# The gating projection's second block product taken apart into seven small ones

## The chip, the cores and the metric

The kernel runs on one NeuronCore of one Trainium2 chip. The metric is the device time of one execution in microseconds (us). Three timed runs of the kernel before gave 791.55, 791.96 and 792.16 us; the median is 791.96 us.

## The reference

A transformer layer over 512 tokens of width 2048: windowed attention with its output projection, then a gated embedding, then a last norm. The attention's inner part is left out here, since neither the code of it nor its place changes.

```python
D_MODEL, SEQ, PLE_DIM = 2048, 512, 256

def rmsnorm(x, g):
    y = x * lax.rsqrt(jnp.mean(x * x, axis=-1, keepdims=True) + EPS)
    return y * g

def reference(...):
    hn = rmsnorm(x, norm_g[0])
    y = swa_mixer(hn, ...)             # ends in (out * silu(gate)) @ w_out, 512x2048 @ 2048x2048
    x = x + y
    emb = p[0] @ ple_proj[0]           # 512x256 @ 256x2048
    g = jax.nn.sigmoid(rmsnorm(x, ple_norm[0]) @ ple_gate[0])   # 512x2048 @ 2048x2048
    x = x + emb * g
    return rmsnorm(x, final_g)
```

## The kernel before, in words

**Precision.** All is fp32. A product of two fp32 tiles is three matmuls (`mm3`, lines 124 to 126): each operand is split into a rounded high part and the rest, and high x high, low x high and high x low are added in PSUM. One matmul has a 128x128 stationary tile of activations and 512 columns of weights.

**Pieces.** A weight matrix is used in pieces of 128x1024 elements (512 KB). A piece is loaded by DMA, ACT casts it into its high part (`bhi`, line 689) and DVE subtracts that for the low part (`blo`, line 690). `Pieces` (object `B`) keeps a list of them in the order of use; `get` issues the loads and splits a few pieces ahead. The raw pieces live in `wraw` (3 buffers, names `braw`) or in `grown` (8 buffers, names `ring` or `grown`), the parts in `whi` and `wlo` (3 buffers each); while the list is between two marks (`FOURTH`) every fourth piece has its parts in a tile called `spare`. The waits on these buffers, and no clock, set when a load or a split really starts.

**Block products.** Both large projections (`w_out`, then `ple_gate`) are cut into two by two blocks and made of seven block products instead of eight. The products have numbers 1 to 7; product 1 is a11 times b11, product 2 is a12 times b21, and the others use sums of blocks. A block product is eight steps `(p, jj, m)` of one piece and twelve matmuls each. The sums of weights that it needs are made ahead in HBM while attention runs, each by one copying DMA on the SP queue and one adding DMA on the POOL queue, a few slots later (`sum_weights`, lines 654 and 652); for `ple_gate` part of them is added in the tile itself ("grow": product 7's piece becomes product 6's, and that product 4's, by an adding DMA of POOL, line 671).

**Small products.** In the `w_out` stage, product 2 and product 4 are themselves seven small block products of a 128-row by 512 by 512 shape. A small product is two steps of one piece and six matmuls each ("m" and "n" in the list `OUT`), and they stand between the larger steps.

**The `ple_gate` stage** is seven whole block products in the order `ORDER_PLE` = 2, 7, 1, 6, 5, 3, 4. Products 1, 6, 5 and 3 add up in the same four PSUM banks (`chain`); product 2's result (copied to `s2` by ACT) and product 7's (`s7`) are joined on DVE by `gate`. The names of a trace are: `g` for the banks, `fhg` and `flg` for the two parts of the activations (made by `Forms` from the transposed quarters `hT`), `e` for the embedding's product, `last` and `low` for the last product's weights, split earlier by `split_last`. `gated` makes the sigmoid (ACT), the product with the embedding and the addition to x (DVE, lines 1271 and 1272) and the square for the last norm (ACT).

**Order.** PE's and SP's instructions stand as the code is written. DVE's, ACT's and POOL's stand so too inside `manual_schedule`; elsewhere the framework's scheduler orders them when the program is built. In the kernel before they are as written from the second product of the `ple_gate` stage on (`written()`).

Lines named below: 113, 107 (split of the earlier weights), 484, 492, 503 (attention's masks on POOL), 525 (the matmul that uses them), 1288 (stores).

Of the kernel before, what the change touches and what calls it, by code (L numbers as in the profile page):

```python
# [55 lines left out]
def trunk_kernel(ctx: ExitStack, tc: tile.TileContext, a: dict):  # L56
# [531 lines left out]
    ORDER_OUT, ORDER_PLE = (1, 7, 2, 6, 5, 3, 4), (2, 7, 1, 6, 5, 3, 4)  # L588
# [11 lines left out]
    def small_piece(kh, jj, i):  # L600
        return block("w_out", 2, 1, jj, 2 * kh + i)
# [23 lines left out]

    small_sum(2, 7, lambda i: small_piece(0, 1, i), lambda i: small_piece(1, 1, i))
# [19 lines left out]
    SUM_REST = 2 * len(copies) + 6 - SUM_START  # L646

    def sum_weights(i):

        if i % 2 == 0 and i // 2 < len(copies):  # L650
            if copies[i // 2]:
                nc.sync.dma_start(*copies[i // 2])
        elif i % 2 == 1 and 0 <= i // 2 - 3 < len(adds):
            nc.gpsimd.dma_start(*adds[i // 2 - 3], accum_op=ALU.add, max_dma_last_dim=8192)

    class Pieces:
# [46 lines left out]
        def ahead(self, i):  # L703

            last = len(self.specs) - 9
            for n in range(max(i, 0), min(i + REACH, last) + 1):
# [7 lines left out]
                if sooner or n <= i + 3:  # L714
                    self._prepare(n)
# [4 lines left out]
        def get(self, i):  # L720
# [3 lines left out]
            if kind in ("seed", "grow"):  # L724
                n = next((n for n in range(i + 1, len(self.specs)) if self.specs[n][2] == key), None)
                if n is not None:
                    self.due.append((i + 6, partial_of(self._prepare, n)))
# [5 lines left out]
    FIRST_RING, LAST_RING, REACH = 4, 68, 9  # L733
    FOURTH = 6, 68
    FINAL_G = 6
# [34 lines left out]
    def small_forms(ahead):  # L770

        v = lambda r, c: gates[2 + c][:, :, r * P : (r + 1) * P]
        v11, v12, v21, v22 = v(0, 0), v(0, 1), v(1, 0), v(1, 1)
        t, t5 = (fg[:, n * 512 : (n + 1) * 512].rearrange("p (k t) -> p k t", k=4) for n in range(2))
        for n, q in enumerate(ORDER_IN):
# [6 lines left out]
            fh, fl = (w[:, n % 2].rearrange("p (k t) -> p k t", k=4) for w in (pTh, pTl))  # L782
# [22 lines left out]
    OUT += SHARED  # L805

    def add_stage(nm, order):
# [23 lines left out]
        def add_embeds(p, jj):  # L831
            if nm == "ple_gate" and p in (1, 5, 3, 4):
                j = jj + 2 * (p in (5, 3))
                B.add("proj", a["ple_proj"].rearrange("(k p) d -> p k d", p=P)[:, :, j * 512 : (j + 1) * 512])

        for p in order:
            for jj in range(2):
                if nm == "ple_gate" and (p, jj) == (4, 0):
                    for v in range(2):
                        at["e", v] = len(B.specs)  # L840
                        add_embeds(p, v)
                at[p, jj] = len(B.specs)
                for m in range(4):
                    if (nm, p) in SUMS:
                        src = summed[nm, p, jj, m]
                    else:
                        src = block(nm, *{1: (1, 1), 2: (2, 1), 3: (2, 2), 6: (1, 1), 4: (2, 1)}[p], jj, m)
                    growing = 7, 6, 4
                    kind = "seed" if p == growing[0] else "grow" if p in growing else "one"
                    B.add(kind, src, (nm, jj, m) if p in growing else None)  # L850
                if p != 4:
                    add_embeds(p, jj)
        return at

    add_stage(inside.nm, ORDER_OUT)
    at_ple = add_stage("ple_gate", ORDER_PLE)

    class Forms:
# [6 lines left out]
        def steps(self, p):  # L865

            self.made[p] = []
            for h in range(2):
# [7 lines left out]
                else:  # L876
                    src, sub = {
                        2: (a12, None), 7: (a21, (a21, a11)), 1: (a11, None), 6: (a21, (a22, a21)),
# [156 lines left out]
    def banks(p, jj, nm):  # L1035
# [3 lines left out]
        tag = ("to" if p == 7 or (nm, p) == ("o", 2) else "sp")[jj]  # L1039
# [7 lines left out]
    def some_later(parts):  # L1047

        for _ in range(-(-len(later) // parts)):
            later.pop(0)()  # L1050

    def unit(p, jj, at, forms, todo):

        ps = banks(p, jj, forms.nm)
        f = forms.made[p]
        first = p not in (6, 5, 3)
        for m in range(4):
            bh, bl = B.get(at[p, jj] + m)
# [5 lines left out]
            some_later(4 - m)  # L1064
            todo()
        return ps

# [40 lines left out]
    ple_first = ple_forms.steps(2)  # L1108
# [38 lines left out]
    def inner_part(p, forms, tags):  # L1147

        x = None
        for q in ORDER_IN:  # L1150
            if q in (1, 7, 2, 4):
                ps = bank(f"o{p}_{q}", tags[q])
# [3 lines left out]
            for i in range(2):  # L1156
# [5 lines left out]
                if i == 1:  # L1162
                    coming.append(partial_of(add_in, p, q, ps))
                yield

    def add_in(p, q, ps):
        whither = {
            1: [((0, 0), -1)], 2: [((0, 0), 1)], 7: [((1, 1), 1), ((1, 0), -1)], 6: [((1, 0), -1)],
            5: [((1, 1), 1)], 3: [((0, 1), 1)], 4: [((1, 0), 1)],
        }[q]  # L1170
        for (r, c), sign in whither:
# [16 lines left out]
    smalls = small_forms(small_made)  # L1188
# [12 lines left out]
    }  # L1201
    extra[7, 0, 2] = extra[7, 1, 0] = [smalls]
# [8 lines left out]
    made, inner, seen = {}, inner_part(4, inside.made, {1: "t", 4: "t", 7: "o", 2: "o"}), 0  # L1211
    inner2, seen2 = inner_part(2, small_made, {1: "t", 7: "t", 2: "o", 4: "o"}), 0
    ahead = {p: out_forms.steps(n) for p, n in zip((1, 7, 6, 5), (7, 6, 5, 3))}
    for at, step in enumerate(OUT):
# [30 lines left out]
        if step == FINAL_G:  # L1245
            nc.sync.dma_start(fg, a["final_g"].partition_broadcast(P))
# [11 lines left out]
    def embed(t, w, tag, c=slice(0, 512)):  # L1258
        e_ps = bank(f"e{t}_{done[t]}", tag)
        for k in range(2):  # L1260
            mm3(e_ps[:, c], pTh[:, k, blk(t)], pTl[:, k, blk(t)], w[0][k][:, c], w[1][k][:, c], k == 0, k == 1)
        return e_ps

    def gated(t, j, zin, z, e_ps, c=slice(0, 512)):
# [7 lines left out]
        nc.vector.tensor_add(xt, xt, z)  # L1272
# [29 lines left out]
    s2, s7 = partial("s2"), partial("s7")  # L1302
    turns = [(kp, 1) for kp in range(4)]

    def gate(p, jj, ps, e):

        zs = []
        for tb in range(2):
            v2, v7 = s2[:, jj, tb], s7[:, jj, tb]
            if p == 2:  # L1310
                nc.scalar.copy(v2, ps[tb])
            elif p == 7:
                nc.scalar.copy(v7, ps[tb])
            elif p == 1:
                nc.vector.tensor_sub(v2, v2, ps[tb])
                zs.append((tb, jj, v2, v2))
# [9 lines left out]
    def gate_later(*v):  # L1326
        zs = gate(*v)
        if zs:
            z, y = zs
            later[:0] = [lambda: (next(z), next(y)), lambda: next(z), lambda: next(y), lambda: (run(z), run(y))]  # L1330

    rooms4 = {}
    early = {(6, 1, 2): 0, (5, 0, 2): 1, (5, 0, 3): 2, (5, 1, 2): 3, (5, 1, 3): 4, (3, 0, 3): 5, (3, 1, 2): 6}
# [10 lines left out]
    for n, p in enumerate(ORDER_PLE[:-1]):  # L1346
        nxt = ple_forms.steps(ORDER_PLE[n + 1])
        if n == 1:
            written()
        for jj in range(2):  # L1350
            calls = iter(range(4))

            def todo():
                k = early.get((p, jj, next(calls)))
                if turns:
                    turn(*turns.pop(0), "t")
                    if not turns:
                        nc.vector.tensor_reduce(ss2, ssq2, axis=AX.X, op=ALU.add)
                        run(rsqrt_mean(rstd2, ss2, D, "r2"))
                    return  # L1360
                next(nxt, None)
                if p == 2:
                    next(nxt, None)
                if k is not None:
                    split_last(k)

# [177 lines left out]
```

## Time and profile before

| what | value |
|---|---|
| median of 3 runs | 791.96 us (791.55 to 792.16) |
| the profiled execution | 791.93 us |
| its span, first to last instruction | 790.2 us |
| PE (TensorE) busy | 780.0 us, 99% |
| PEld (weight load) busy | 652.3 us, 83% |
| DVE (VectorE) busy | 612.9 us, 78% |
| ACT (ScalarE) busy | 499.6 us, 63% |
| POOL (GpSimd) busy | 175.8 us, 22% |
| mean granted TensorE clock | 0.996 |

Engines: PE is the matrix engine, PEld its weight loads, SP the engine that issues most DMAs. Times are us from the start of the span unless marked ns. Line numbers (L690) are those of the kernel before. "out<-in" names the tiles written and read, xN counts instructions. A busy matmul row is 390 ns long because matmuls are pipelined; how often one starts is read from the starts. An `idle before` time names what ended the wait. The `ple_gate` stage begins at 604.3 us and PE's last matmul starts at 781.0 us.

### The profile page before, as it was taken

The page shows a single profiled execution, that of the slowest core. Times are in us where ns is not written, and L with a number is a line of the kernel's source. Part 1 is how long each engine was busy: PE and PEld are TensorE (multiplying, and loading weights), DVE is VectorE, ACT ScalarE, POOL GpSimd, SP SyncE. Part 2 cuts the span into 40 slices and gives each one's busy share as a digit, 9 for nine tenths or more (in the row PEclk, how much of TensorE's full clock was granted, in tenths as well). Part 3 has the DMA queues.
Part 4 walks back from the last instruction along what each step waited for, and adds up shares of the span by engine and source line. Part 5 has one row for each costly group of instructions (what it writes and reads, how often), then busy time and mean ns, then how long its engine had stood idle before and what let it go on. Part 6 is the DMA issues. An engine that isn't in the chain of part 4 may idle for free.

```text
span 790.2 us, 11240 instructions
## 1 busy us (share of the span) xinstructions
PE 780.0 (99%) x3738; PEld 652.3 (83%) x3738; DVE 612.9 (78%) x1043; ACT 499.6 (63%) x1016; POOL 175.8 (22%) x382
## 2 busy tenths in 40 slices
PE   9999999999999999999999999999999999999995
PEld 8888888888888888888888888888888888888885
DVE  4445478887877788687887799999788757999886
ACT  5641376666666666565666656767679756667755
POOL 0012413554344414442243200100000120200000
PEclk9999999999999999999999999999999999999998
DMA  8781999999999998999998687997783995885433
GB/s 334 279 227 39 322 267 295 269 290 269 328 253 290 255 281 212 268 259 276 290 271 220 159 313 257 271 381 264 239 297 105 370 225 207 164 217 197 169 107 107
DMA packets 48490, 194.41 MB, mean 246 GB/s; under 512 B 7296, under 2 KB 7936, under 8 KB 42704
## 3 DMA queue, kind: packets, MB, share of 16 engines
q1 hardware_dynamic: 39456, 148.94, 53.2%
q0 software_dynamic: 8688, 44.36, 29.4%
q8 instruction: 29, 0.48, 0.3%
q10 hardware_dynamic: 288, 0.39, 0.2%
q14 instruction: 29, 0.24, 0.1%
HBM read 187.85 MB, written 70.31 MB: 327 GB/s over the span
## 4 chain that ended last, share of the span: by engine, by line
PE 98%; DMA 0%; DVE 0%; ACT 0%; issue 0%; DVEq 0%
PE gps L124 7%; PE gps L125 7%; PE gps L126 7%; PE qps L124 7%; PE qps L125 7%; PE qps L126 7%; PE o L126 6%; PE o L124 6%; PE o L125 6%; PE g L126 6%; PE g L125 6%; PE g L124 6%; PE s L401 2%; PE o L523 2%; PE vps L228 2%; PE pt L479 2%
## 5 line engine op out<-in xcount | busy, mean ns | idle before, releaser
L124 PE MATMUL gps<-xh,whi 128*128 128x512 f32 x256 | 100.7, 393 | 0.0
L125 PE MATMUL gps<-xl,whi 128*128 128x512 f32 x256 | 100.1, 391 | 0.0
L126 PE MATMUL gps<-xh,wlo 128*128 128x512 f32 x256 | 100.0, 391 | 0.0
L503 POOL TENSOR_SCALAR_AFFINE_SELECT own<-r 64x256 fp32r<-64x256 f32 x96 | 62.4, 650 | 162.3 <-ACT r L484 80.2
L113 DVE TENSOR_TENSOR wlo<-wraw,whi 128x1024 fp32r<-128x1024 f32 x60 | 73.5, 1226 | 24.7 <-ACT whi L107 23.2
L124 PE MATMUL qps<-xh,whi 128*128 128x512 f32 x224 | 87.8, 392 | 0.0
L125 PE MATMUL qps<-xl,whi 128*128 128x512 f32 x224 | 87.5, 391 | 0.0
L126 PE MATMUL qps<-xh,wlo 128*128 128x512 f32 x224 | 87.5, 390 | 0.0
L461 ACT ACTIVATE t<-t,sm 128x129 f32<-128x129 f32 x128 | 50.6, 397 | 51.2 <-DVE sm L452 47.9
L124 PE MATMUL g<-bhi,fhg 128*128 128x512 f32 x192 | 75.3, 392 | 0.0
L126 PE MATMUL g<-bhi,flg 128*128 128x512 f32 x192 | 74.9, 390 | 0.0
L125 PE MATMUL g<-blo,fhg 128*128 128x512 f32 x192 | 74.8, 389 | 0.0
L107 ACT CAST whi<-wraw 128x1024 fp32r<-128x1024 f32 x60 | 62.2, 1037 | 15.7 <-DMA wraw<-in_w_q 9.5
L689 ACT CAST bhi<-braw 128x1024 fp32r<-128x1024 f32 x44 | 46.4, 1057 | 36.1 <-PE g L126 20.5
L690 DVE TENSOR_TENSOR blo<-braw,bhi 128x1024 fp32r<-128x1024 f32 x44 | 54.1, 1229 | 18.5 <-ACT bhi L689 18.3
L690 DVE TENSOR_TENSOR blo<-ring,bhi 128x1024 fp32r<-128x1024 f32 x48 | 58.3, 1223 | 6.6 <-ACT bhi L689 6.2
L689 ACT CAST bhi<-ring 128x1024 fp32r<-128x1024 f32 x48 | 50.2, 1050 | 20.4 <-PE o L126 16.8
L126 PEld LDWEIGHTS gps<-xh,wlo 128*128 128x128 f32 x256 | 48.1, 188 | 10.5
L484 ACT CAST r<-pt 128x256 fp32r<-128x256 f32 x64 | 23.8, 372 | 51.3 <-PE pt L479 50.9
L124 PEld LDWEIGHTS gps<-xh,whi 128*128 128x128 f32 x256 | 48.1, 188 | 9.0
L125 PEld LDWEIGHTS gps<-xl,whi 128*128 128x128 f32 x256 | 48.1, 188 | 8.7
L671 POOL DMA_DIRECT2D grown<-in_ple_gate x16 | 13.7, 854 | 176.4 <-DMA grown<-ple_gate 119.8
(265 smaller groups left out, 1988.7 us busy)
## 6 DMA issues: line engine op xcount, KB each, us to landing
w_out<-in_w_out POOLq DMA_DIRECT2D x32, 512.0 KB, 8.7
wraw<-in_w_gate_in SPq DMA_DIRECT2D x32, 512.0 KB, 7.3
ring<-w_out SPq DMA_DIRECT2D x32, 512.0 KB, 5.9
wraw<-in_w_q SPq DMA_DIRECT2D x28, 512.0 KB, 8.1
braw<-in_ple_gate SPq DMA_DIRECT2D x24, 512.0 KB, 4.0
ring<-in_w_out SPq DMA_DIRECT2D x18, 512.0 KB, 4.5
w_out<-in_w_out SPq DMA_DIRECT2D x16, 512.0 KB, 9.6
w_out<-w_out SPq DMA_DIRECT2D x16, 512.0 KB, 13.6
```

The source lines that it names most:

```text
L107: nc.scalar.copy(hi, self.raw[i])
L113: nc.vector.tensor_sub(lo, raw, hi.bitcast(F32))
L124: nc.tensor.matmul(ps, sh, mh, start=first, stop=False, skip_group_check=more)
L125: nc.tensor.matmul(ps, sh, ml, start=False, stop=False, skip_group_check=more)
L126: nc.tensor.matmul(ps, sl, mh, start=False, stop=last, skip_group_check=more)
L228: nc.tensor.matmul(v_ps[t], h[:, c], both[:, :, 256:512], start=f, stop=e, skip_group_check=True)
L401: nc.tensor.matmul(s_ps[:, u, : 2 * n], st, key[:, :, first : first + n], start=True, stop=True)
L461: nc.scalar.activation(su, su, AF.Exp, bias=sm[:, u : u + 1], accum_out=sm[:, 2 + u : 3 + u])
L484: nc.scalar.copy(r[:, 0], PT[i])
L503: nc.gpsimd.affine_select(out=cols(own[places[g % 2 ^ low]]), in_=cols(r[here, low].bitcast(F32)), pattern=[[sign * QB, 2], [0, GROUP], [s ...
L689: nc.scalar.copy(hi, raw)
L690: nc.vector.tensor_sub(lo, raw, hi.bitcast(F32))
```

## The change

Product 2 of the `ple_gate` stage is taken out of the order of the large products and is made of seven small ones, as product 2 of `w_out` is already. Its fourteen "m" steps stand between the steps of products 7 (second half), 6 and 5. With that:

- eight more sums of weights are made in HBM (`small_g`, two each for small products 7, 5, 6 and 4); four sums (`ple_gate` product 5, second half) leave the time of attention and are issued in the `w_out` stage (`LATE_AT`), and the first half of product 5's sums goes to the head of the list.
- the small products' results are added by DVE in a tile `c11`, which is the tile of `final_g` (`fg`); product 1's negative is put there first by ACT. `final_g` is loaded later for that reason, in product 3.
- the embedding's steps ("e") of products 1 and 5 come later in the list.
- for x tiles (2, 2), (2, 3), (3, 2), (3, 3) the addition of the gated embedding to x is an adding DMA of POOL, no longer a DVE instruction; their squares come eight steps later.
- pieces are loaded up to seven steps ahead with at most three waiting; `spare` serves until piece 99.
- `written()` is called after product 3 only, so that the scheduler orders DVE, ACT and POOL in the whole stage up to the last product.

```diff
-    ORDER_OUT, ORDER_PLE = (1, 7, 2, 6, 5, 3, 4), (2, 7, 1, 6, 5, 3, 4)
+    ORDER_PLE = (1, 7, 6, 5, 3, 4)
...
+    large_sum("ple_gate", 5, (0,))
     small_sum(2, 7, lambda i: small_piece(0, 1, i), lambda i: small_piece(1, 1, i))
...
+    small_sum("g", 7, lambda i: gate_piece(0, 1, i), lambda i: gate_piece(1, 1, i))
+    small_sum("g", 5, lambda i: gate_piece(0, 0, i), lambda i: gate_piece(0, 1, i))
...
+    small_sum("g", 6, lambda i: small["g", 7, i], lambda i: gate_piece(0, 0, i))
...
-    large_sum("ple_gate", 5, (0,))
+    small_sum("g", 4, lambda i: small["g", 6, i], lambda i: gate_piece(1, 0, i))
...
+    LATE_SUMS = len(copies)
     large_sum("ple_gate", 5, (1,))
+    late_sums = [(c, v) for c, v in zip(copies[LATE_SUMS:], adds[LATE_SUMS:])]
+    del copies[LATE_SUMS:], adds[LATE_SUMS:]
...
+    LATE_AT = ((1, 0, 0), (1, 0, 2)), (8, 10), (9, 11), (10, 12)
...
-    FIRST_RING, LAST_RING, REACH = 4, 68, 9
-    FOURTH = 6, 68
+    FIRST_RING, LAST_RING, REACH, AHEAD, GROW = 4, 68, 9, 7, 12
+    FOURTH = 6, 100
...
+    PLE = [(1, n // 4, n % 4) for n in range(8)]
+    for n in range(8):
+        PLE.append((7, n // 4, n % 4))
+        if n >= 4:
+            PLE.append("m")
+    for n in range(8):
+        PLE += [(6, n // 4, n % 4), "m"]
+    PLE += [(5, 0, 0), ("e", 1, 0), "m", (5, 0, 1), "m", (5, 0, 2), (5, 0, 3), ("e", 1, 1), (5, 1, 0), (5, 1, 1)]
+    PLE += [(5, 1, 2), ("e", 5, 0), (5, 1, 3), ("e", 5, 1)]
+    PLE += [(3, 0, m) for m in range(4)] + [("e", 3, 0)] + [(3, 1, m) for m in range(4)] + [("e", 3, 1)]
...
+    BY_DMA = {(2, 2), (2, 3), (3, 2), (3, 3)}
...
-        nc.vector.tensor_add(xt, xt, z)
+        if (t, j) in BY_DMA:
+            nc.gpsimd.dma_start(xt, z, accum_op=ALU.add)
+        else:
+            nc.vector.tensor_add(xt, xt, z)
...
+    def put_in(p, q, ps):
+        for (r, c), sign in WHITHER[q]:
+            v = c11[:, c, r]
+            if sign > 0:
+                nc.vector.tensor_add(v, ps, v)
+            else:
+                nc.vector.tensor_sub(v, v, ps)
...
+    inner = inner_part("g", gate_made, {1: "t", 7: "t", 2: "o", 4: "o"}, put_in)
+    for at, step in enumerate(PLE, len(OUT)):
+        if step == "m":
+            next(inner)
...
+            if step == FINAL_G:
+                nc.sync.dma_start(fg, a["final_g"].partition_broadcast(P))
```

The order of instructions at two places of the stage. Pieces are numbered through the program; the `ple_gate` stage begins with piece 68 in both kernels. In the changed one, pieces 76 to 87 are product 7 and the first small steps (81, 83, 85 and 87 are small), 88 to 103 product 6 (odd ones small), 104 to 117 product 5 (106 and 108 small; 105, 111, 115 and 117 embeddings), and 118 to 127 product 3.

DVE, from the joining of product 6's second half (`s2<-g1,s7`) on, before; `blo105` to `blo107` are low parts of product 5's pieces, `flg3` those of product 3's activations, `low1` is a piece of the last product:

```order
L1318 TENSOR_TENSOR s2_6392<-g1_1_0_6888,s7_6393 128x512
L1318 TENSOR_TENSOR s2_6392<-g1_1_1_6889,s7_6393 128x512
L882 TENSOR_TENSOR hT2_6206<-hT2_6206,hT0_5988 128x4x256
L690 TENSOR_TENSOR blo105_7188<-braw105_7163,bhi105_7187 128x1024
L895 TENSOR_TENSOR flg3_00_7205<-hT2_6206,fhg3_00_7204 128x512
L690 TENSOR_TENSOR blo106_7211<-braw106_7185,bhi106_7210 128x1024
```

The same place on DVE now; `ig_4` is a small product's bank, `fg` the tile of `c11`, `e0_105` the embedding's bank:

```order
L1362 TENSOR_TENSOR s2_6423<-g1_1_0_6543,s7_6424 128x512
L1362 TENSOR_TENSOR s2_6423<-g1_1_1_6544,s7_6424 128x512
L711 TENSOR_TENSOR blo105_7122<-braw105_7069,bhi105_7121 128x1024
L1345 TENSOR_TENSOR fg_5050<-ig_4_7089,fg_5050 128x512
L930 TENSOR_TENSOR flg3_01_7245<-hT2_6223,fhg3_01_7244 128x512
L711 TENSOR_TENSOR blo106_7134<-braw106_7100,bhi106_7133 128x1024
L930 TENSOR_TENSOR flg3_10_7311<-hT3_6330,fhg3_10_7310 128x512
L711 TENSOR_TENSOR blo107_7157<-braw107_7119,bhi107_7156 128x1024
L1303 TENSOR_TENSOR fg_5050<-e0_105_0_7160,fg_5050 128x512
L1303 TENSOR_TENSOR fg_5050<-e1_105_0_7167,fg_5050 128x512
L711 TENSOR_TENSOR blo108_7177<-braw108_7131,bhi108_7176 128x1024
L1307 TENSOR_TENSOR x1_0_5046<-x1_0_5046,fg_5050 128x512
```

Four further instructions lead in the changed kernel up to the low part of piece 110: `blo109`, a second addition to x, `low1` and `blo110`; all but the addition have 128x1024 elements. What moved: small results and the embedding of product 1 now stand among product 5's splits.

SP's queue at product 7's pieces, before (`grown` are the seeds of product 7, `braw84` the first piece of product 1):

```order
L679 DMA braw75_6517<-in_ple_gate 128x1024
L679 DMA grown78_6519<-ple_gate_7_0_2_788 128x1024
L679 DMA grown79_6544<-ple_gate_7_0_3_789 128x1024
L679 DMA grown80_6567<-ple_gate_7_1_0_792 128x1024
L679 DMA grown81_6593<-ple_gate_7_1_1_793 128x1024
L679 DMA grown82_6615<-ple_gate_7_1_2_794 128x1024
L679 DMA grown83_6639<-ple_gate_7_1_3_795 128x1024
L679 DMA braw84_6721<-in_ple_gate 128x1024
```

SP's queue at the same place now:

```order
L700 DMA grown80_6591<-ple_gate_7_1_0_802 128x1024
L700 DMA braw81_6593<-in_ple_gate 128x1024
L700 DMA grown82_6637<-ple_gate_7_1_1_803 128x1024
L700 DMA braw83_6639<-in_ple_gate 128x1024
L700 DMA grown84_6682<-ple_gate_7_1_2_804 128x1024
L700 DMA braw85_6684<-small_g_7_0_794 128x1024
L700 DMA grown86_6730<-ple_gate_7_1_3_805 128x1024
L700 DMA braw87_6732<-small_g_7_1_795 128x1024
L700 DMA braw89_6765<-small_g_6_0_800 128x1024
```

Here the small steps' pieces (`small_g`, and raw blocks of `in_ple_gate`) stand between the seeds, in the three `braw` buffers.

More of the change, by code (lines that the diff above doesn't have):

```diff
@@ L831, in add_embeds @@
         def add_embeds(p, jj):
[L832 to L841, printed above, removed]
-                at[p, jj] = len(B.specs)
[L843 to L852, printed above, removed]
@@ L1344, in split_last @@
         B.split_last(k, rooms4[(k - 1) // 2][:, (k - 1) % 2 * WE : ((k - 1) % 2 + 1) * WE], lo)
-    for n, p in enumerate(ORDER_PLE[:-1]):
-        nxt = ple_forms.steps(ORDER_PLE[n + 1])
-        if n == 1:
-            written()
[L1350 to L1360, printed above, removed]
+    FINAL_G = 3, 1, 0
```

197 lines of the change are left out of this document (137 added, 60 removed).

## The prediction

> **What bounds the kernel now.** I read the page's busy times and slices first, then the chain that ended last, then PE's waits.
>
> ```profile
> span 790.2 us, 11240 instructions
> PE 780.0 (99%) x3738; PEld 652.3 (83%) x3738; DVE 612.9 (78%) x1043; ACT 499.6 (63%) x1016; POOL 175.8 (22%) x382
> PE   9999999999999999999999999999999999999995
> DVE  4445478887877788687887799999788757999886
> PE 98%; DMA 0%; DVE 0%; ACT 0%; issue 0%; DVEq 0%
> ```
>
> PE is busy in every slice but the last, and the chain is PE for 98% of the span. The waits of PE over the whole run are only these two (line, releaser, total us, times, longest):
>
> ```profile
> PE warm_ps L145 <- PEq L1534: 0.8, 1, 0.8
> PE qps L216 <- ACT xh L199: 0.4, 1, 0.4
> ```
>
> So the time is the number of matmuls times their spacing, plus about 9 us behind the last one. Work taken off another engine gains nothing while this holds; a matmul taken away gains its spacing, unless PE now waits. The profiled execution took 791.93 us (790.2 of span, 1.7 around it), as good as the median of 791.96, so the sum needs no correction.
>
> **The change, part by part. 1: PE.** The stage loses one product of eight steps by twelve matmuls, 96, and gets fourteen small steps by six, 84. The order confirms it: twelve matmuls fewer in the program, nothing else of PE's removed. Embedding matmuls only move. The spacing, from the timeline in product 2, first and last of 68 matmuls in a row:
>
> ```profile
> 619.53 0.39 PE L125 MATMUL g<-blo,fhg 128*128 128x512 f32 x1
> ...
> 634.72 0.39 PE L126 MATMUL g<-bhi,flg 128*128 128x512 f32 x1
> ```
>
> (634.72 - 619.53) / 67 = 0.2267 us, so 12 x 0.2267 = 2.72 us less. That is the whole gain.
>
> The Trainium skill (TensorE: Matmul & The Clock Gate, section "Wait — 56ns, not 53.3ns?") gives 215.7 ns from start to start for a warm matmul of 512 columns; by it the gain would be an estimated 2.59 us. The trace differs by 11 ns, and the trace decides.
>
> **2: DVE and ACT in products 6 and 5.** This is where the gain can be lost. A small step hands PE six matmuls, 6 x 0.2267 = 1.36 us of work, yet costs a whole piece: a cast on ACT and a subtraction on DVE. Before, a large piece fed PE for 2.72 us. Windows, with busy time of PE, PEld, DVE, ACT and POOL, then granted clock, DMA share and GB/s:
>
> ```profile
> 480.00:520.00 40.00, 40.00 (x178) 33.16 (x177) 37.32 (x43) 28.46 (x40) 4.88 (x4) 1.00 0.89 258
> 520.00:560.00 40.00, 40.00 (x179) 33.13 (x178) 37.54 (x45) 27.82 (x40) 0.00 (x0) 1.00 0.86 304
> ...
> 640.00:680.00 40.00, 40.00 (x178) 33.16 (x177) 27.10 (x28) 22.78 (x30) 3.44 (x5) 1.00 0.72 198
> 680.00:720.00 40.00, 40.00 (x178) 33.13 (x178) 37.50 (x44) 27.36 (x35) 5.06 (x6) 1.00 0.84 206
> 720.00:750.00 30.00, 30.00 (x134) 24.87 (x133) 27.28 (x32) 22.18 (x34) 0.00 (x0) 1.00 0.54 183
> ```
>
> Room on DVE is at 640 to 680 (27.1 of 40). At 680 to 720 it is 94% busy already. But so it is in 480 to 560, the `w_out` stage with the same mixture of large and small steps, and PE waits nowhere there. What a DVE instruction costs in a row, from its timeline:
>
> ```profile
> 686.11 0.68 DVE L1271 TENSOR_TENSOR s<-e,s 128x512 f32<-128x512 f32 x1
> 686.82 0.69 DVE L1272 TENSOR_TENSOR x<-x,s 128x512 f32<-128x512 f32 x1
> 687.43 0.68 DVE L895 TENSOR_TENSOR flg<-hT,fhg 128x512 fp32r<-128x512 f32 x1
> 688.03 1.22 DVE L690 TENSOR_TENSOR blo<-grown,bhi 128x1024 fp32r<-128x1024 f32 x1
> 689.17 1.22 DVE L882 TENSOR_TENSOR hT<-hT 128x1024 f32<-128x1024 f32 x1
> 690.30 1.22 DVE L690 TENSOR_TENSOR blo<-grown,bhi 128x1024 fp32r<-128x1024 f32 x1
> ```
>
> Back to back the starts are 0.60 us apart behind a 512-column one (687.43 to 688.03) and 1.14 behind a 1024-column one (688.03 to 689.17), 0.71 where one needs the result ahead of it (686.11 to 686.82). That is less than the printed durations, which overlap.
>
> From `blo80` to `blo117` the new order has 44 instructions of 1024 columns and 41 of 512: 44 x 1.14 + 41 x 0.60 = 74.8 us (81.9 if the printed durations added up). PE's work for those pieces is 23 steps of twelve and 14 of six, 360 matmuls, 81.6 us. On average DVE is 92% busy, and there is no room left if the durations did not overlap.
>
> The tightest place is the DVE list shown above. Both `s2` joinings need PE's end of product 6 (pieces 102 and 103), and from there nine 512 and seven 1024 instructions stand ahead of piece 110's step: 9 x 0.60 + 7 x 1.14 + 0.2 for chained pairs = 13.6 us, 14.8 by printed durations. PE has 66 matmuls meanwhile, 14.96 us. The margin is 1.2 us, or about nothing by the upper bound. I take the lower, since the rows quoted show these shapes in just this sequence.
>
> ACT has 1.05 us per cast more, and is busy 27.4 of 40 where it is densest. Its idle time is mostly waiting for a buffer of PE's, and its casts go 0.96 us apart:
>
> ```profile
> ACT bhi L689 <- PE g L126: 30.3, 27, 1.7
> 693.67 1.05 ACT L689 CAST bhi<-braw 128x1024 fp32r<-128x1024 f32 x1 [1.15 <-issue]
> 694.63 1.04 ACT L697 CAST spare<-grown 128x1024 fp32r<-128x1024 f32 x1
> ```
>
> Walking the pieces one after the other with these durations, the least lead of a split over PE is 0.6 to 1.0 us, at pieces 103 to 110, and 2 to 5 us elsewhere. I take no stall; bounds 0 and 3 us (three splits late by about one duration each; below zero is excluded, since PE has no wait there to lose).
>
> **3: Loads.** Issues with size and median us to landing:
>
> ```profile
> braw<-in_ple_gate SPq DMA_DIRECT2D x24, 512.0 KB, 4.0
> grown<-in_ple_gate POOLq DMA_DIRECT2D x16, 512.0 KB, 7.0
> fg<-in_final_g SPq DMA_DIRECT2D x1, 1024.0 KB, 7.0
> x<-in_x POOLq DMA_DIRECT2D x4, 512.0 KB, 10.5
> ```
>
> A `braw` buffer is loaded, cast and subtracted in 4.0 + 1.05 + 1.22 = 6.3 us; in product 6 only the small pieces use them, but in product 5 all do: pieces 104 to 110 are 72 matmuls in seven steps, so three feed PE for 72 x 3 / 7 x 0.2267 = 7.0 us on average, though 106 to 108 (6 + 12 + 6) for 5.4 alone. That is enough, barely: a landing of 7 us instead of 4 would make PE wait. I cost it at nothing, bounds 0 and 3 us in all, together with part 2 and not on top of it, as both delay the same split. `fg` lands in 7.0 us and is used in the tail, over 16 us after its issue between `braw127` and `braw128`: 0, and at worst 1 us for the load queued behind it.
>
> **4: Additions to x.** Four DVE instructions of 0.69 us become DMAs of POOL that only squares eight steps later (16 us or more) need. Landing taken like `x<-in_x`, 10.5 us: hidden. If not, the tail is late by up to 1 us.
>
> **5: Sums behind attention.** Twelve large-product sums stay, eight small ones come in, and four go to the `w_out` stage: net four copies (SP) and four additions (POOL) of 512 KB more before 446 us.
>
> ```profile
> 140.00:180.00 40.00, 40.00 (x206) 33.73 (x205) 32.78 (x74) 27.08 (x77) 20.99 (x50) 1.00 1.01 285
> 180.00:220.00 40.00, 40.00 (x201) 33.56 (x200) 33.00 (x74) 27.41 (x76) 15.23 (x32) 1.00 1.02 293
> 300.00:340.00 40.00, 40.00 (x202) 33.52 (x200) 30.08 (x65) 24.02 (x67) 18.80 (x43) 1.00 0.93 248
> 420.00:446.00 26.00, 26.00 (x128) 21.78 (x127) 19.48 (x40) 16.90 (x44) 9.39 (x22) 1.00 0.80 190
> q1 hardware_dynamic: 12462, 65.42, 47.5%
> q0 software_dynamic: 5072, 33.08, 45.3%
> POOL w_out L654 <- DMA w_out<-w_out: 11.8, 3, 9.1
> ```
>
> The queue rows are those of 60 to 440 us: q1 takes 0.475 x 380 / 65.42 = 2.76 us of the sixteen engines for a MB, q0 5.20. The four sums are 2.1 MB on each: 5.8 + 10.9 = 16.7 us. Free there is 1 - 0.928 - 0.003, 7% of 380, 26 us. It fits on average, though not at 140 to 220, where the share is 1.0; there each sum pushes the rest. PE has kept busy at a share of 1.02, so a full DMA alone does not stop it; the weights' loads (`wraw`, landing in some 7 us) have that much reserve. I take 0; the upper bound is the part falling in full stretches (about 160 of 346 us): 16.7 x 160 / 346 = 7.7 us. The two copies and two additions in the `w_out` stage meet a share of 0.86 to 0.89: 0.
>
> **Sum.** -2.72 and nothing else on the path: 791.93 - 2.72 = 789.21, by the median 789.24, so 789.2 us with a span of 787.5. A change under 0.2% (1.6 us, to 790.4) is about what a measurement can't tell from none.
>
> **Rivals.**
> (A) DVE or the three `braw` buffers bound PE at pieces 103 to 117, with stalls of 0.5 to 3 us: 789.7 to 792.2, centre 790.5. For it: margins of 1 us, and 14.8 us by printed durations against 14.96. Against it: 480 to 560.
> (B) Slower: DMA traffic in attention makes a weight load late. Price up to 7.7 - 2.7, about 797, decided once a load that lands in some 7 us comes after its cast is due. For it: the 1.01 and 1.02; against it: 0.93 and 0.80 later, where buffers catch up, and POOL's wait for copies, 11.8 us, that cost nothing.
> (C) Slower: one wait of PE of 4 us or more, for instance a seed of product 6 whose adding DMA is late, lets its clock fall. These rows are from behind the last matmul (781.0):
>
> ```profile
> 783.00:785.00 2.00, 0.00 (x0) 0.00 (x0) 1.74 (x7) 1.58 (x5) 0.00 (x0) 0.58 0.00 0
> 785.00:787.00 2.00, 0.00 (x0) 0.00 (x0) 0.33 (x2) 0.17 (x1) 0.00 (x0) 0.50 0.98 321
> ```
>
> The granted clock is 0.58 and then 0.50 some 2 to 4 us after the end. A wait of 4 us would cost itself and, with 2 to 4 us at half speed, 1 to 2 more: 4 + 1.5 - 2.7, about 794.8. The Trainium skill (TensorE: Matmul & The Clock Gate, Part 1, "What's actually happening") says the clock halves after an idle window of some 3.4 us and that as long a busy one restores it; by its figure the restart is an estimated 1.7 us more, and the rows agree with the fall.
> (D) The tail is later by 1 us or so (squares, `fg`): 790.2.
> That the change doesn't do what it says is excluded by the order.
>
> **How the numbers follow.** Forecast, stall under 0.5 us: 0.58, its own range 788.8 to 789.9, faster. (A) 0.23: 0.07 faster (stalls up to 1.1 us), 0.12 same, 0.04 slower (stalls beyond its bound, over 4.3 us). (B) 0.08: 0.01 same, 0.07 slower. (C) 0.04, slower. (D) 0.05, split 0.02 and 0.03 between faster and same. The rest, 0.02, unknown: 0.01 same, 0.01 slower. Together faster 0.67, same 0.17, slower 0.16. The range leaves out B, C and A's worst: 788.6 to 792.0, the low end 0.6 under the forecast for the scatter of runs.
>
> **What would show it.** Right: 12 matmuls fewer, PE busy near 777.3 us, no wait of PE for `bhi` or `blo` in the stage; DVE at 9 in the slices of products 6 and 5; attention's DMA share a few hundredths higher with no PE wait; about 9 us behind the last matmul. Wrong on 2 or 3: PE waits on DVE's `blo` at pieces 103 to 117, with DVE busy throughout (2) or its splits waiting for `braw` (3). Wrong on 5: PE or ACT waits on `wraw` between 140 and 220 us. The forecast falls if PE's waits add up to over 1.2 us.

## The result, and the profile after

The changed kernel took 799.36 us in the median of six runs (796.47 to 802.61), against 792.10 (791.55 to 792.26) of the kernel before: a ratio of 1.0091, 95% interval 1.0079 to 1.0103. It is slower, where 789.2 was forecast, and its runs lie 6 us apart where those of before lie within 0.7. The profiled execution took 797.25 us, so the sums below account for one of the faster executions, and the median is 2.1 us above it.

The page of the changed kernel, the lines that answer to those shown of before:

```profile
span 795.5 us, 11324 instructions
PE 780.5 (98%) x3726; PEld 649.8 (82%) x3726; DVE 622.5 (78%) x1056; ACT 506.7 (64%) x1025; POOL 179.6 (23%) x394
PE   9999999999998999999999999999999999999995
DVE  4545478887867788787886798999798988998695
PE 80%; issue 12%; DMA 2%; POOL 2%; DVE 2%; ACT 0%; POOLq 0%; DVEq 0%; SPq 0%; ACTq 0%
```

The twelve matmuls are gone (3726), but PE was not 2.72 us less busy. A part of that is a stretch of attention at a lower clock, shown below, which kept PE busy 1.6 us longer. One slice of PE, the thirteenth (238 to 259 us), is an 8: that is in attention, 350 us ahead of the stage that was rewritten. PE's waits over the whole run (line, releaser, total us, times, longest):

```profile
PE o L523 <- DVE r L492: 2.0, 1, 2.0
PE warm_ps L145 <- PEq L1617: 0.9, 1, 0.9
PE g L125 <- DVE blo L711: 0.8, 1, 0.8
PE e L125 <- DVE blo L711: 0.7, 1, 0.7
PE qps L216 <- ACT xh L199: 0.5, 1, 0.5
PE g L124 <- ACT bhi L710: 0.3, 1, 0.3
PE o L525 <- POOL own L503: 0.2, 1, 0.2
```

Two are old, the other five are new: two in attention, three in product 3 of the gating stage.

**Where the time went.** From the timelines of PE I took the first matmul of the `w_out` stage, the first of the gating stage and the last one of all. The rows of the gating stage's begin, before and after:

```profile
604.31 0.48 PE L124 MATMUL g<-bhi,fhg 128*128 128x512 f32 x1
```

```profile
608.60 0.48 PE L124 MATMUL g<-bhi,fhg 128*128 128x512 f32 x1
```

| part of the profiled execution, us | before | after | difference |
|---|---|---|---|
| up to the first matmul of `w_out` | 451.80 | 456.09 | +4.29 |
| `w_out` stage | 152.51 | 152.51 | 0 |
| gating stage, first to last matmul | 176.67 | 177.12 | +0.45 |
| behind the last matmul, to the end of the execution | 10.95 | 11.53 | +0.58 |
| sum | 791.93 | 797.25 | +5.32 |

DVE's last instruction ends 4.3 us behind the start of PE's last one in both, so the 0.58 lies behind it, where only the last stores are left.

**Attention.** The wait, from the cause to PE: a cast of ACT, DVE's subtraction and selection behind it, and PE's matmuls, from the three engines' timelines.

```profile
236.89 1.05 ACT L107 CAST whi<-wraw 128x1024 fp32r<-128x1024 f32 x1 [5.63 <-DMA wraw<-in_w_gate_in]
```

```profile
237.97 1.23 DVE L113 TENSOR_TENSOR wlo<-wraw,whi 128x1024 fp32r<-128x1024 f32 x1 [6.39 <-ACT whi L107]
...
240.89 0.41 DVE L492 TENSOR_TENSOR r<-pt,r 128x256 fp32r<-128x256 f32 x1
```

```profile
238.94 0.36 PE L523 MATMUL o<-r,V 128*128 128x256 f32 x1
241.35 0.39 PE L523 MATMUL o<-r,V 128*128 128x256 f32 x1 [2.05 <-DVE r L492]
241.99 0.39 PE L525 MATMUL o<-own,DV 128*128 128x256 f32 x1 [0.25 <-POOL own L503]
```

ACT waits 5.6 us for a raw weight before it can cast it, and everything that ACT and DVE have queued behind, `r` among it, waits too. Windows of the same place (PE, PEld, DVE, ACT, POOL, then granted clock, DMA share, GB/s):

```profile
238.00:242.00 4.00, 1.70 (x9) 0.93 (x7) 3.19 (x7) 1.74 (x8) 1.85 (x3) 1.00 1.02 334
242.00:246.00 4.00, 4.00 (x12) 3.22 (x13) 3.59 (x11) 3.31 (x11) 2.36 (x7) 0.57 1.09 434
246.00:250.00 4.00, 4.00 (x22) 3.37 (x22) 1.90 (x4) 1.37 (x4) 0.95 (x5) 1.00 1.13 312
```

After the pause the granted clock is 0.57 for one window. Nine intervals of matmuls from 242.47 to 246.12 take 3.65 us instead of 9 x 0.2267 = 2.04, so 1.6 us are lost to the clock. The pause itself costs 2.8: from 238.94 to the matmul at 242.47 are 3.53 us, and the same five matmuls further on take 0.71 (249.00 to 249.71). Together that is 4.4. Attention lost 4.56, since its first matmul of L479 started 0.27 us earlier than before (105.73 against 106.00 us), and 0.1 stays without a name.

**Gating stage.** Twelve matmuls less should have made it 173.95; it is 177.12, so 3.17 us were lost. ACT's timeline there:

```profile
731.58 0.63 ACT L1310 ACTIVATE s<-x 128x512 f32<-128x512 f32 x1 [2.86 <-DMA x<-s]
...
737.25 0.63 ACT L1310 ACTIVATE s<-x 128x512 f32<-128x512 f32 x1 [1.84 <-DMA x<-s]
...
738.80 0.63 ACT L1310 ACTIVATE s<-x 128x512 f32<-128x512 f32 x1 [0.82 <-DMA x<-s]
739.34 0.19 ACT L1310 ACTIVATION_READ_ACCUMULATOR s<-x 128x1 f32 x1
739.43 1.98 ACT L710 CAST bhi<-braw 128x1024 fp32r<-128x1024 f32 x2
```

Three squares wait 5.5 us for the new adding DMAs (`x<-s`), and the casts of the next pieces stand behind them. PE waits for what these casts lead to, at 733.9, 735.2 and 741.8 us; by the starts of the matmuls these places cost 2.6 of the 3.17 us. Most of the rest is lost without the adding DMAs too (0.37 us in run 1, 174.32); "The prediction, step by step" shows on what.

### The profile page after: what moved, and what is told of

Same layout as the page of the kernel before. It is cut to its first block, busy times and chain, and to the rows that moved or that the text cites. A ratio compares the mean times of both kernels' runs of the same rounds, so it can differ in the third digit from the quotient of the medians.

```text
span 795.5 us, 11324 instructions
## 1 busy us (share of the span) xinstructions
PE 780.5 (98%) x3726; PEld 649.8 (82%) x3726; DVE 622.5 (78%) x1056; ACT 506.7 (64%) x1025; POOL 179.6 (23%) x394
## 4 chain that ended last, share of the span: by engine, by line
PE 80%; issue 12%; DMA 2%; POOL 2%; DVE 2%; ACT 0%; POOLq 0%; DVEq 0%; SPq 0%; ACTq 0%
PE gps L124 7%; PE gps L125 7%; PE gps L126 7%; PE qps L124 7%; PE qps L126 7%; PE qps L125 7%; PE o L124 5%; PE o L125 5%; PE o L126 5%; PE s L401 2%; PE o L523 2%; PE vps L228 2%; PE pt L479 2%; POOL grown L692 2%; PE i L124 1%
## 5 line engine op out<-in xcount | busy, mean ns | idle before, releaser
L124 PE MATMUL gps<-xh,whi 128*128 128x512 f32 x256 | 101.1, 395 | 0.0
L124 PE MATMUL qps<-xh,whi 128*128 128x512 f32 x224 | 87.7, 392 | 0.0
L711 DVE TENSOR_TENSOR blo<-braw,bhi 128x1024 fp32r<-128x1024 f32 x43 | 52.5, 1226 | 13.0 <-ACT bhi L710 12.9
L125 PE MATMUL g<-blo,fhg 128*128 128x512 f32 x148 | 58.0, 392 | 0.8 <-DVE blo L711 0.8
L124 PE MATMUL g<-bhi,fhg 128*128 128x512 f32 x148 | 58.2, 393 | 0.3 <-ACT bhi L710 0.3
L126 PE MATMUL g<-bhi,flg 128*128 128x512 f32 x148 | 57.7, 390 | 0.0
L124 PEld LDWEIGHTS gps<-xh,whi 128*128 128x128 f32 x256 | 48.5, 189 | 9.3
L126 PEld LDWEIGHTS qps<-xh,wlo 128*128 128x128 f32 x224 | 42.1, 188 | 9.1
```

The source lines that it names most:

```text
L124: nc.tensor.matmul(ps, sh, mh, start=first, stop=False, skip_group_check=more)
L125: nc.tensor.matmul(ps, sh, ml, start=False, stop=False, skip_group_check=more)
L126: nc.tensor.matmul(ps, sl, mh, start=False, stop=last, skip_group_check=more)
L711: nc.vector.tensor_sub(lo, raw, hi.bitcast(F32))
```

## The experiments

All were timed side by side with the kernel before (791.88 to 792.12 us). The table gives the median, the ratio with its interval, and from each profiled execution the first matmul of `w_out` and the length of the gating stage.

| run | us | ratio (95%) | `w_out` begins | gating stage |
|---|---|---|---|---|
| before | 791.9 to 792.1 | 1 | 451.80 | 176.67 |
| the change | 799.36 | 1.0091 (1.0079 to 1.0103) | 456.09 | 177.12 |
| 1. additions on DVE | 795.99 | 1.0058 (1.0040 to 1.0076) | 455.95 | 174.32 |
| 2. four sums left out | 793.08 | 1.0013 (1.0005 to 1.0022) | 451.89 | 178.29 |
| 3. both | 789.91 | 0.9975 (0.9966 to 0.9983) | 451.87 | 174.32 |
| 4. the sums alone | 799.61 | 1.0079 (1.0050 to 1.0108) | 459.40 | 176.67 |
| 5. before, crowded | 798.89 | 1.0096 (1.0081 to 1.0110) | 456.75 | 176.67 |
| 6. sums sooner | 811.83 | 1.0250 (1.0237 to 1.0263) | 473.26 | 174.59 |
| 7. eight late sums | 790.44 | 0.9985 (0.9977 to 0.9994) | 452.39 | 174.30 |
| 8. eight late, paced | 790.34 | 0.9981 (0.9972 to 0.9990) | 452.55 | 173.99 |
| 9. squares last | 793.80 | 1.0024 (1.0014 to 1.0034) | 452.33 | 177.24 |
| 9. DMAs beside | 789.61 | 0.9970 (0.9958 to 0.9981) | 451.80 | 174.86 |

The column `w_out` begins has a difference in it that is older than attention. Attention's first matmul of L479 starts at 106.00 us before, at 108.02 with the sums alone, and at 106.58 and 106.75 in runs 7 and 8; these differences arise in the program's first 10 us. The first matmul of L124, for instance, starts at 6.51 us before and at 7.84, 7.11 and 7.30 in these three. Less that, attention lost 4.6 us in the change, 5.6 with the sums alone, and 0.0 in runs 7 and 8.

**Theory and rival.** Two causes: the list of sums makes loads late in attention, and the adding DMAs hold up ACT. The rivals: DVE has no room in product 5; the order of the list and not its pace; the DMAs' traffic and not the wait.

**1. Additions back on DVE.**

```diff
-    BY_DMA = {(2, 2), (2, 3), (3, 2), (3, 3)}
+    BY_DMA = set()
```

> The changed kernel with the four additions to x back on DVE (nothing on POOL there). Theory 1 (ACT's squares wait for the adding DMAs, 5.5 us in the trace, and casts stand behind them; that is PE's stall of 2.8 us at 733 to 742): the stall goes, the stretch from the first matmul of the gating stage to the last falls from 177.1 to about 174.3 us, and about 2.8 us of the median go: 799.4 becomes 796 to 797, with the attention's losses and their scatter still there. Rival (DVE has no room at these pieces): four more DVE instructions of 0.69 us make PE wait longer, 0 to 2.8 us slower than the changed kernel.

795.99 us, 3.4 less than the change. The gating stage took 174.32, 2.8 less than in the change and as expected, with no wait of PE's matmuls in it. DVE had room for the four instructions. The losses in attention stayed, at other places this time (180, 202 and 332 us).

**2. Four sums left out.**

```diff
-    small_sum("g", 6, lambda i: small["g", 7, i], lambda i: gate_piece(0, 0, i))
...
-    small_sum("g", 4, lambda i: small["g", 6, i], lambda i: gate_piece(1, 0, i))
-    for n in range(2):
-        copies.append(None)
-        adds.append(None)
...
-                raw = {1: (0, 0), 2: (1, 0), 3: (1, 1)}.get(q)
+                raw = {1: (0, 0), 2: (1, 0), 3: (1, 1), 6: (0, 0), 4: (1, 0)}.get(q)
```

> The changed kernel without the four sums of small products 6 and 4 and the two empty places: 60 places in the list, as before the change. Their steps read a raw block of the same size instead, so the output is not the reference's. Theory 2 (the additional sums make attention's weight loads late; PE waits 2 us and its clock falls): no wait of PE between 100 and 446 us, the gating stage begins near 604.3 instead of 608.6 us, the scatter of 796 to 803 shrinks to under 1 us, and the median falls by 4 to 7 us to 792 to 795, the adding DMAs' 2.8 us still in it. Rival (not the number but the new order, product 5's first half at the head, brings the load late): stays at 797 to 800.

793.08 us (791.90 to 794.09), 6.3 less than the change. Attention is as before (`w_out` begins at 451.89), though product 5's first half still stands at the head of the list: the order is not to blame. The scatter is 2.2 us, more than the 1 expected. The gating stage lost more than in the change, 178.29, as a longer pause there was followed by matmuls 0.43 us apart between 732.8 and 735.8.

**3. Both.**

> Both of the first two edits: additions on DVE, and the four sums left out (the output is not the reference's). If theories 1 and 2 hold and are all there is: 791.96 - 2.72 plus at most 0.5 us, 789.2 to 789.7, PE without a wait over 0.5 us. If DVE is short of room: 790.5 to 792. If the order of the sums is to blame: 793 or more.

789.91 us, 0.2 above the range expected: the two effects add up, 3.4 + 6.3 = 9.7 of which 9.45 came. PE's waits in the whole run, and two windows of it:

```profile
PE warm_ps L145 <- PEq L1612: 0.9, 1, 0.9
PE qps L216 <- ACT xh L199: 0.3, 1, 0.3
```

```profile
710.00:720.00 10.00, 10.00 (x46) 8.29 (x45) 10.00 (x12) 9.22 (x14) 0.00 (x0) 1.00 0.66 206
...
730.00:740.00 10.00, 10.00 (x46) 8.29 (x45) 10.00 (x12) 6.93 (x12) 0.00 (x0) 1.00 0.69 214
```

DVE is busy in every moment of these windows, and no matmul is listed as waiting. The narrow margin was enough, or nearly: small waits show on the weight loads (PEld), and "The prediction, step by step" has their rows.

**4. The sums alone, in the kernel before.** The changed kernel's list of sums with its late ones, while the gating stage is as before; nobody reads the eight small sums.

```diff
+    large_sum("ple_gate", 5, (0,))
     small_sum(2, 7, lambda i: small_piece(0, 1, i), lambda i: small_piece(1, 1, i))
...
+    small_sum("g", 7, lambda i: gate_piece(0, 1, i), lambda i: gate_piece(1, 1, i))
+    small_sum("g", 5, lambda i: gate_piece(0, 0, i), lambda i: gate_piece(0, 1, i))
...
+    small_sum("g", 6, lambda i: small["g", 7, i], lambda i: gate_piece(0, 0, i))
...
-    large_sum("ple_gate", 5, (0,))
+    small_sum("g", 4, lambda i: small["g", 6, i], lambda i: gate_piece(1, 0, i))
...
```

> The kernel before with the changed kernel's list of sums alone (eight small sums that nothing reads, four late ones issued in the w_out stage); the gating stage stays as before. Theory 2: slower than before by what attention loses in the changed kernel, 4 to 8 us, 796 to 800, with PE waiting for DVE r or ACT between 200 and 250 us and a scatter of several us. Rival (attention's stall is chance or comes of the gating stage's code): 792.0 as before.

799.61 us (793.23 to 801.51), with the gating stage at 176.67 as before. PE and ACT wait as in the change:

```profile
PE o L523 <- DVE r L492: 2.9, 2, 2.0
...
ACT whi L107 <- DMA wraw<-in_w_gate_in: 4.9, 1, 4.9
ACT whi L107 <- DMA wraw<-in_w_q: 4.1, 1, 4.1
```

**5. Number or pace.** The list is dealt out in slots: 8 of them ahead of attention's 64 blocks, the rest over the blocks. The change made them 130 over the blocks instead of 118. This run keeps the kernel before and its own sums, and adds twelve empty slots at the end:

```diff
+    copies += [None] * 6
+    adds += [None] * 6
     SUM_START = 8
...
```

> The kernel before with its own sums, but six empty places (twelve slots) at the end of the list: the same sums in 138 slots' pace, 9% closer together, and done earlier. If the pace is the cause: slower, 794 to 800, with late loads of wraw between 180 and 260 us. If only the four additional sums' bytes count: 792, as before.

798.89 us, as slow as the change, with not one byte more to move in all. So it is the pace. Counted in the timelines up to 240 us, SP had issued 33 copies and POOL 28 additions before; 35 and 30 in the change and in this run; 33 and 28 with four sums left out. Two of each are 2 x 0.524 MB x 2.76 = 2.9 and 2 x 0.524 x 5.20 = 5.5 us of DMA time, in a stretch whose share is about 1.0 already (0.97 to 1.02 before, from 100 to 260 us). The landing of the `wraw` loads between 100 and 446 us, before, after, and in this run, in that order:

```profile
DMA to landing us min/median/max: 4.6/7.6/18.4
```

```profile
DMA to landing us min/median/max: 4.6/9.2/18.2
```

```profile
DMA to landing us min/median/max: 3.8/11.0/22.5
```

**6. Sums sooner: a miss.** The change with additions on DVE, and the more of the list ahead of attention's blocks:

```diff
-    SUM_START = 8
+    SUM_START = 20
```

> All sums of the changed kernel, additions to x on DVE, but 20 places of the list stand ahead of attention's blocks instead of 8 (there the DMA share is 0.60 to 0.84), so that attention has 118 places, as before the change. If the rate of sums in attention's full stretches is the cause: no wait of PE there, 789.5 to 790.6, as with the four sums left out (789.9). If it is the number of sums, wherever they stand: 794 to 797, as with the additions on DVE alone (796.0).

811.83 us. The share of 0.60 at 60 to 100 us was no room. Windows, and ACT's waits from 60 to 446 us:

```profile
60.00:100.00 40.00, 40.00 (x184) 33.27 (x183) 17.62 (x30) 8.69 (x13) 8.47 (x17) 1.00 0.63 187
100.00:140.00 40.00, 25.90 (x102) 20.07 (x101) 16.85 (x43) 15.76 (x44) 12.58 (x28) 0.84 1.02 269
```

```profile
ACT whi L107 <- DMA wraw<-in_w_q: 27.0, 5, 7.9
```

Up to 100 us SP had issued 11 copies instead of 5, and up to 120 us 10 loads of `wraw` instead of 13: the transfers lie ahead of the loads just where attention begins. Of the 27.0 us of ACT's wait 14.5 lie ahead of 100 us, where PE stays busy (before, the same row has 7.5 in all). PE waits between 106 and 140 us only, and for nothing in the rest of attention, at a DMA share of 0.94 to 1.02 up to 420 us. Neither of the two expectations held; attention's pace was that of before, and it was the burst in front of it that hurt.

**7. Eight late sums.** All sums are made, additions on DVE; both halves of product 5's sums are issued in the `w_out` stage.

```diff
-    large_sum("ple_gate", 5, (0,))
     small_sum(2, 7, lambda i: small_piece(0, 1, i), lambda i: small_piece(1, 1, i))
...
-    large_sum("ple_gate", 5, (1,))
+    large_sum("ple_gate", 5)
...
-    LATE_AT = ((1, 0, 0), (1, 0, 2)), (8, 10), (9, 11), (10, 12)
+    LATE_AT = ((1, 0, 0), (1, 0, 2)), ((1, 1, 0), (1, 1, 2)), ((7, 0, 1), (7, 0, 3)), ((7, 1, 1), (7, 1, 3)), ((6, 0, 2), (6, 1, 0)), (8, 10), (9, 11), (10, 12)
```

> All sums, additions to x on DVE; both halves of ple_gate product 5's sums are issued in the w_out stage (eight instead of four), and 62 places are left in attention. Theory: attention as before; the w_out stage takes 16.7 us of DMA time more in 152 us, a share of about 0.97 instead of 0.86 to 0.90, and its pieces come a little later: 789.7 to 791. Rival (a share near 1 makes the w_out stage wait as attention did): 792 to 795 with PE waiting for bhi or blo between 450 and 608 us.

790.44 us: faster than both kernels by the median, with all the work done, though only by 0.15% of before and with a slowest execution of 793.63. The `w_out` stage took 153.40 us, 0.9 more, in the profiled execution; up to its end weight loads waited 1.4 us for `blo`, where they wait 0.2 before.

**8. The same, paced.** The two empty places go, and 60 places remain, as before the change:

```diff
+    small_sum(4, 6, lambda i: small[4, 7, i], lambda i: large_piece(0, 0, i))
     large_sum("ple_gate", 7, (1,))
-    small_sum(4, 6, lambda i: small[4, 7, i], lambda i: large_piece(0, 0, i))
     small_sum("g", 4, lambda i: small["g", 6, i], lambda i: gate_piece(1, 0, i))
-    for n in range(2):
-        copies.append(None)
-        adds.append(None)
```

> All sums made, additions to x on DVE, eight late sums, and the two empty places taken out (small sums 4,6 moved ahead of product 7's second half instead), so that attention has 60 places at the pace of the kernel before. If the pace is what counts: no wait of PE in attention and less scatter than with 62 places (789.6 to 793.6): median 789.8 to 790.6. If the w_out stage's own loss is larger than thought: 791 or more.

790.34 us (789.52 to 791.84), 0.9981 of before. The scatter went down from 4.0 to 2.3 us. Of the 2.72 us of the forecast 1.8 came by the medians. In the profiled execution the 0.75 us by which `w_out` begins late were there at 106 us already, and attention adds nothing. The `w_out` stage is back at 152.51, though its DMA share was no lower, and the gating stage took 173.99: 2.68 us less than before. Windows of this run, ahead of them those of before, at 500 to 550 us:

```profile
500.00:550.00 50.00, 50.00 (x222) 41.43 (x221) 48.13 (x57) 34.92 (x49) 3.65 (x3) 1.00 0.95 309
```

```profile
500.00:550.00 50.00, 50.00 (x222) 41.43 (x221) 47.66 (x56) 35.54 (x49) 4.51 (x4) 1.00 1.05 341
```

So a share above 1 is borne in the `w_out` stage, and PE stays busy.

**9. The wait or the traffic.** First the four squares were written later, in the kernel with four sums left out:

```diff
-    SLOW = 8
+    SLOW = 99
```

> The changed kernel with the four sums left out (its output is not the reference's) and the additions to x by DMA kept, but the squares of the four tiles are written down after the last product has begun; two of them now stand on ACT behind the cast of piece 127, the other two ahead of the cast of piece 122. Theory (ACT waits in its squares, and casts stand behind): PE's stall shrinks or goes, 790 to 791.8 instead of 793.1. Rival (the adding DMAs themselves take the room from the loads of the pieces): 793 as it was.

793.80 us, no shorter than run 2, as the rival had it; yet it decides little. Only two of the squares had really moved. The other two still waited 3.3 us ahead of casts, and PE's pause was one place of 1.3 + 0.8 us; another cast waited 3.4 us for a `braw` load, which rather spoke for the traffic. So the traffic was put to the test by itself: both edits of run 3, and beside the additions on DVE four DMAs of POOL that nobody waits for.

```diff
             nc.vector.tensor_add(xt, xt, z)
+        if (t, j) in {(2, 2), (2, 3), (3, 2), (3, 3)}:
+            nc.gpsimd.dma_start(tc.dram_tile([P, 512], F32, name=f"beside_{t}_{j}"), xt)
```

> The kernel with additions on DVE and the four sums left out (789.9; its output is not the reference's), plus four DMAs of 256 KB on POOL at the places of the adding ones, from the same x tiles into HBM, that nobody waits for. If ACT's wait for the landing is the whole cost of the adding DMAs: 789.9 to 790.3, PE without a wait. If their traffic is the cost, because braw loads come late beside them: 791 to 793, with casts waiting for braw and PE for bhi or blo at 725 to 740 us.

789.61 us: as fast as without them. Casts did wait for `braw` loads between 720 and 745 us (3.1 us, 2.6 of it at once), but no matmul of PE did, and run 8, which has none of these DMAs, shows 5.3 us of such waits there. The gating stage of the profiled execution is 0.54 us longer than in run 3; the late starts lie at 695 to 708 us, ahead of the first of these DMAs (724). These DMAs go from x into HBM, where the adding ones read and write x itself, so a part of the traffic is not tested; the traffic that was costs nothing, and the wait is what remains.

## The prediction, step by step

- **What bounds the kernel, and part 1 (PE): right.** In the paced version, where neither matmuls nor weight loads wait in it, the gating stage is 2.68 us shorter; 2.72 was the sum.
- **Part 2 (DVE and ACT): right in the main.** No wait of PE's matmuls for DVE at pieces 103 to 117 in runs 3 and 8 or with the DMAs beside, and the back-to-back distances were the ones to take. In the runs with additions on DVE it even carried four instructions that the sum had taken off. But the margin, 1.4 us by the sum's own terms (14.96 - 13.6) and not 1.2, was used up at a few pieces, by DVE and the loads together: PE's weight loads wait for `blo`, and with the DMAs beside, where most is lost, two of these subtractions had waited 1.4 and 1.2 us for casts, and the casts 2.3 and 1.0 us for `braw` loads (691 and 703 us). These rows are the weight loads' only waits between 640 and 760 us, in run 3 and with the DMAs beside; run 8 has none:

```profile
PEld g L125 <- DVE blo L706: 0.6, 2, 0.3
```

```profile
PEld g L125 <- DVE blo L706: 0.9, 3, 0.4
PEld e L125 <- DVE blo L706: 0.4, 1, 0.4
```

  The matmuls behind them start 0.31 to 0.39 us apart instead of 0.23, and the gating stage is 174.32 and 174.86 us long instead of the 173.99 of run 8. So rival (A) is out as the cause of the slowdown, and is worth 0.3 to 0.9 us where it shows.
- **Part 3 (loads): right in the main.** Casts waited for `braw`, and PE lost by it no more than the little named under part 2.
- **Part 4 (additions to x): wrong.** The step was "only squares eight steps later (16 us or more) need". The landing was 5.6 us in the median, shorter than the 10.5 allowed for; but the squares stood where the scheduler had put them. ACT's order of the changed kernel, which was set when the program was built, has them among the casts of pieces 120 to 122 (rows of the order with the waits in brackets):

```
L1310 ACTIVATE s7_6424,ssq3_5054<-x1_2_5048 128x512 [waits DMASW0_49]
L1301 ACTIVATE s7_6424<-s7_6424,rstd2_6417 128x512 [waits DVE_49]
L710 CAST bhi120_7433<-braw120_7383 128x1024 [waits DMAHW1_49,PE_49,Activation_49]
L1310 ACTIVATE s7_6424,ssq3_5054<-x1_2_5048 128x512 [waits DMASW1_49]
L710 CAST bhi121_7461<-braw121_7411 128x1024 [waits DMAHW2_49,PE_49,Activation_49]
L1310 ACTIVATE s7_6424,ssq3_5054<-x1_3_5049 128x512 [waits DMASW2_49,DVE_49]
L1310 ACTIVATE s7_6424,ssq3_5054<-x1_3_5049 128x512 [waits DMASW3_49,DVE_49]
L710 CAST bhi122_7490<-braw122_7431 128x1024 [waits DMAHW3_49,PE_49,Activation_49]
```

  The trace has them in the same order, from 731.58 to 739.43 us. The "eight steps" stood in the code, in a part whose order the code does not set. And the place was looked for at the tail, not at the casts behind. The price was 3.4 us by the medians of the change and of run 1, 3.2 by those of runs 2 and 3, and 2.8 by the lengths of the gating stage; 0 was taken, with 1 as the bound.
- **Part 5 (sums): wrong, and the larger part.** The step was "It fits on average", and the value 0. Four sums were priced by their bytes over all of attention; what counted was that all sums came 10% closer together (run 5). It was rival (B), given 0.08, with a bound of 7.7 us, or 5 net of the gain; the loss was 6.3 us by run 2, inside that bound. So the size lay within what was thought possible, and the chance was put too low. The row that spoke against it, PE busy at a share of 1.02, was read the wrong way: at such a share nothing is left, and a PE that does not wait there shows that the margin was not yet used up.
- **Rival (C): the mechanism right, the threshold wrong.** It took "one wait of PE of 4 us or more" for the clock to fall; a wait of 2.05 us, in a window in which PE was busy for 1.7 of 4 us, was enough here, and the 1.6 us that followed were as estimated.
- Two terms were taken at nothing, each with its own reason why it would stay hidden, and the chances gave 0.16 to slower. Both reasons failed.

## What to carry to other kernels

In this kernel, where the DMA share was 1 and nothing waited yet, the bytes of a background transfer did not give its price: look at how closely transfers are spaced, and at what stands in the queue of the engine whose load comes late. Where a scheduler sets the order, read on the built order where a consumer of a new DMA stands and what is behind it; the code's "eight steps later" is no promise. Work that an engine was spared (DVE here) gains nothing while that engine is not the one waited for, and the wait it buys is paid in full. A list of PE's waits with nothing in it is not yet proof of room: read the weight loads' waits too.

## What the runs showed of the hardware

**The clock can fall after a short pause.** The rows of 238 to 250 us: after a pause of 2.4 us between two starts the granted clock was 0.57 in the next 4 us, and nine intervals between matmuls, most of them 0.43 us, took 3.65 us. The Trainium skill (TensorE: Matmul & The Clock Gate, Part 1, "What's actually happening") has the clock fall after an idle window of some 3.4 us and come back after a busy one as long. The length of the slow stretch agrees; the pause was shorter than that window, and here the measurement decides. Not every pause does it, and the length alone does not tell: 1.13 and 1.26 us between starts in run 2 (729 to 732 us) were followed by matmuls 0.43 us apart, while 1.65 and 1.26 in the first kernel of run 9 (735 to 738 us) were not. In the changed kernel those at 733 to 736 us, 0.73 and 1.26 us, left the clock at 1.00:

```profile
733.00:736.00 3.00, 1.90 (x8) 1.02 (x7) 2.75 (x4) 2.41 (x4) 0.85 (x1) 1.00 0.92 221
736.00:739.00 3.00, 3.00 (x14) 2.30 (x13) 3.00 (x3) 0.92 (x3) 0.00 (x0) 1.00 0.89 238
```

**With the sums closer together the time became uncertain.** The changed kernel took 796.5 to 802.6 us, and the kernel with the sums alone 793.2 to 801.5, where the kernel before stays within 1 us over the runs timed beside any one of them. Where in attention PE waited differed between the profiled executions (106 to 140, 181, 203, 241, 245 or 332 us). A part of a difference can be older than attention: with the sums alone 2.0 of the 7.6 us by which `w_out` begins late arose in the first 10 us. Why one execution loses 2 us and another 8 is open.
